# Input projection of a hybrid encoder block: bank split, lasting value tiles, unit order and weight timing changed

## The chip, the cores and the metric

The kernel runs on 1 core of one Trainium2 chip. The metric is the device time of one execution in microseconds (us), and the time of a kernel is the median of several runs. Five engines work beside each other, each with its own queue that it follows strictly in order: PE (TensorE) multiplies matrices into PSUM banks, DVE (VectorE) and ACT (ScalarE) read PSUM and SBUF, POOL (GpSimd) works on SBUF, and SP (SyncE) mostly issues DMA transfers. POOL issues some DMAs too. A semaphore holds an instruction back until what it needs is there, and whatever stands behind it on its engine is held back with it.

## The reference, cut to what matters

```python
def reference(x, mem, positions, norm_mix_g, w_in, ...):           # x: 2048 x 1024
    xn = rmsnorm(h, norm_mix_g[l])
    proj = xn @ w_in[l]                                            # 1024 -> 2560
    q, k, v, u, y = jnp.split(proj, [512, 1024, 1536, 2048], axis=-1)
    q = rope(q.reshape(B, S, 8, 64), positions)
    k = rope(k.reshape(B, S, 8, 64), positions)
    attn = dilated_mixture_attention(q, k, v)                      # three windows and dilations
    uc = centred_depthwise_conv(u, conv_w[l], conv_b[l])           # width 4
    rec = bidirectional_rglru(uc, rg_a_w[l], ...) * jax.nn.gelu(y) # forward and backward scans
    h = h + jnp.concatenate([attn, rec], axis=-1) @ w_out[l]
    h = h + memory_cross_attention(rmsnorm(h, ...), rmsnorm(memf, ...), wq, wk, wv, wo)
    hid = jnp.square(jax.nn.relu(rmsnorm(h, ...) @ w_mlp_in[l]))
    h = h + hid @ w_mlp_out[l]
    return rmsnorm(h, norm_final_g)
```

The change touches the first part: the projection to q, k, v, u and y, the rotary step, and the convolution and recurrence that run beside it.

## The kernel before, in words

Matrices are multiplied in three passes. Each f32 operand is split into a rounded high part (written by ACT, such as `wh`, `xh`) and the remainder (`wl`, `xl`: operand minus high part), and a product is high x high, high x remainder and remainder x high (`mm3`, lines 119 to 121 by the profile). A helper keeps no result that is remainder x remainder.

The sequence is worked in two blocks of 1024 positions, each in two halves of 512 (`th`). The 2560 output columns are cut into ten units of 256 columns: two of u, two of y, and v, k and q with two each (`n2` 0 and 1, that is heads 0 to 3 and 4 to 7). Block 0 makes u and y first. Then block 1 is loaded, keys and values of the memory are made (`memory_kv`), and block 1 makes u, y and its six units of v, k and q. Then x of block 0 is loaded again (`x_block` through the three `wraw` buffers, 16 pieces) and block 0 makes its six units of v, k and q. After that attention begins, head by head, with loads of q, k and v from DRAM (`load_head`; POOL issues those of q and k).

- A u, y, k or q unit is four groups of 24 matmuls of 512 columns (`out_unit`), each into one PSUM bank. A v unit (`v_unit`) also fills four banks, with 48 matmuls of 256 columns each. Banks `m0`, `m1` and `b` hold two each and are taken in turn, six in all; the recurrence's gates use the two banks of `a`.
- DVE evacuates. k and q go through `rope` (lines 376 to 386: four products that read the banks, then two sums, then remainders `rl`, with ACT's `rh` between), and `rh` and `rl` are stored to DRAM from two buffers each. v is scaled by the row norms (line 451) and put as f16 high part (ACT, line 456) and remainder (DVE, line 457) into the tile `vb`, one buffer, whose two columns of ones POOL writes each time (line 454), and stored.
- Weights come by DMA in four pieces of a unit, ACT makes `wh` (line 225), and POOL and DVE make `wl` (line 226) for every other piece. Of `wh` and `wl` there are buffers for two units. The v units of block 1 also sum the squares of their weights' columns over the same pieces (`vss`, `vsq`), which they need before their first bank can be evacuated.
- The recurrence (`lru`) is a generator of 64 pieces: convolution of a chunk (`conv`: POOL takes the first tap at line 489, DVE three more at line 491), the gates of a direction (`gates`: six matmuls into two banks of `a`, then tanh, tanh, exp, tanh and square on ACT, two steps on DVE), `forward` (square root on ACT, products and a scan on DVE, line 531) and `backward` (scan at line 536, sum of the directions by POOL at line 539, product with gelu(y) by DVE at line 544). From block 1's y units on, each step of a unit (four a unit) draws pieces: `due` grows by 1.3 a step, and one piece is drawn for each whole.

A scheduler puts each engine's instructions in order from the written order, priorities and buffers; the queues follow that order. At the change from projection to attention the eight banks are given out again (`psum_phase`): the first attention scores use banks `a`, of which one was a projection bank `m1` before.

Of the kernel before, what the change touches and what calls it, by code (L numbers as in the profile page):

```python
# [24 lines left out]
VW = 130  # L25
# [14 lines left out]
def hybrid_block(ctx: ExitStack, tc: tile.TileContext, prm, x, xT, mem, memT, pos, masks, w_in, gate_w,  # L40
# [35 lines left out]
    turn = {"mm": 0, "mmb": 0}  # L76
# [25 lines left out]
    nhalf = small("nhalf", [P, 4])  # L102
    pool.memset(nhalf, -0.5)
    ones = small("ones", [P, 1])
    pool.memset(ones, 1.0)
    all1 = small("all1", [P, P])
    pool.memset(all1, 1.0)
    dsc = small("dsc", [P, 4])
    hpi = small("hpi", [P, 1])
# [94 lines left out]
    psum_phase("psum1", m0=2, m1=2, a=2, b=2)  # L204
    sh = ExitStack()
    with ExitStack() as s12:
# [10 lines left out]
        def unit_steps(src, r, sums=None):  # L217
            for kk in range(2):
# [3 lines left out]
                for k in range(0, 4, 2):  # L222
# [3 lines left out]
                    (dve if k else pool).tensor_tensor(l[:, k:k + 2, :], t, f32(h[:, k:k + 2, :]), op=ALU.subtract)  # L226
# [36 lines left out]
        def memory_kv(p1):  # L263
# [12 lines left out]
            for c in range(8):  # L276
                if c % 2 == 0 and c > 0:
                    W = unit_w((w_ck if c < 4 else w_cv)[(c % 4) // 2])
                o = ps("mm")
# [15 lines left out]
                else:  # L295
                    t = ps("b")
# [93 lines left out]
        def out_unit(W, X, c, th):  # L390
            o = ps("mmb")
# [40 lines left out]
        def v_unit(W, X, B, n2, step, sums):  # L432

            for th in range(2):
                for m2 in range(2):
                    o = ps("mmb")
# [16 lines left out]
                    vb = p2.tile([P, 8, VW], F16, tag="vb", name="vb", bufs=1)  # L453
                    pool.memset(vb[:, :, 64:66], 1.0)
# [8 lines left out]
        def lru(lr):  # L463
# [12 lines left out]
            def conv(ct, zc):  # L476
# [12 lines left out]
                pool.tensor_scalar(uc, u[:, 0:512], cw[:, ct, 0:1], cb[:, ct:ct + 1], op0=ALU.mult, op1=ALU.add)  # L489
# [44 lines left out]
            def backward(ct, c):  # L534
# [4 lines left out]
                pool.tensor_tensor(hf, hf, ti, op=ALU.add)  # L539
# [1026 lines left out]
```

## Time and profile before

| what | value |
|---|---|
| time, median of 3 runs | 2870.84 us (2866.83 to 2875.58) |
| time of the profiled execution | 2870.64 us |
| its span, first to last instruction | 2868.9 us |
| granted TensorE clock, mean | 0.952 |
| PE busy in the span | 2585.6 us (90%) |
| DVE busy | 2027.9 us (71%) |
| ACT busy | 1285.1 us (45%) |
| POOL busy | 1256.8 us (44%) |

The projection fills the first 704 us of the span. In what follows this part is cut into stretches at places that the trace shows: 0 to 189 us (block 0's u and y, the memory, block 1's u), 189 to 245.5 us (block 1's y), 245.5 to 615 us (block 1's v, k, q, the reload of x, and block 0's v, k, q and second v), 615 to 704 us (block 0's second k and q until attention runs). A row of a timeline gives the start, the duration, the engine, line and operation, the tiles as out<-in, and in square brackets the idle time of that engine before it and what ended it. A row of groups gives the count, the busy time and the mean in ns, then the idle time ahead of the group. Buffer numbers are left out of names.

### The profile page before, as it was taken

To read this page: it belongs to the slowest core of one execution; us is meant where nothing else is said; L and a number is where in the kernel's file an instruction comes from. 1 tells how busy PE (TensorE), PEld (TensorE's weight loads), DVE (VectorE), ACT (ScalarE), POOL (GpSimd) and SP (SyncE) were. 2 spreads that over 40 slices of the span, in tenths; PEclk is the share of its full clock that TensorE was granted. 3 is DMA by queue.
4 is the path that set the end of the run, shared out by engine and by line. 5 is a ranking of instruction groups with operands and counts; after the bars stand their busy time and mean duration, and the time that the engine had idled before them with its cause. 6 is when DMAs were issued, how large, how long until landed. Compare 5 with 4: busy or idle time off the path is not lost. (4 is left out here: it accounts for less than half of the span.)

```text
span 2868.9 us, 40008 instructions
## 1 busy us (share of the span) xinstructions
PE 2585.6 (90%) x14104; PEld 2186.2 (76%) x14104; DVE 2027.9 (71%) x3376; ACT 1285.1 (45%) x2366; POOL 1256.8 (44%) x884
## 2 busy tenths in 40 slices
PE   8899785884889998999997999899998999999997
PEld 6778675774889998787875788778886777777876
DVE  7547676764778878546578544665548999999997
ACT  6438545452556666335433333433333333333342
POOL 2222121211544442451145555646656766666662
PEclk9999897987889999899998999999999999999999
DMA  6433344336677784653243333343335222212213
GB/s 214 144 125 98 116 113 141 101 106 186 180 184 210 201 206 124 202 170 102 97 159 121 108 113 107 113 144 109 109 114 205 71 84 81 81 67 89 77 49 118
DMA packets 258045, 368.43 MB, mean 128 GB/s; under 512 B 85683, under 2 KB 132019, under 8 KB 254773
## 3 DMA queue, kind: packets, MB, share of 16 engines
q1 hardware_dynamic: 253556, 338.62, 37.4%
q0 software_dynamic: 4288, 27.27, 3.8%
q8 instruction: 111, 1.82, 0.3%
q14 instruction: 90, 0.73, 0.1%
HBM read 251.19 MB, written 114.63 MB: 128 GB/s over the span
## 5 line engine op out<-in xcount | busy, mean ns | idle before, releaser
L1299 ACT ACTIVATE c<-raw 128x512 fp32r<-128x512 f32 x162 | 101.8, 632 | 274.0 <-PE m L120 137.4
L1149 ACT ACTIVATE wh<-wr 128x512 fp32r<-128x512 f32 x128 | 80.9, 632 | 288.9 <-PE m L120 145.9
L1150 POOL TENSOR_TENSOR wl<-wr,wh 128x512 fp32r<-128x512 f32 x96 | 144.7, 1508 | 146.3 <-ACT wh L1149 146.3
L757 ACT ACTIVATE sm<-sm,obp 128x256 f32<-128x256 f32 (+1 forms) x384 | 161.4, 467 | 46.2 <-DVE obp L754 40.0
L1150 DVE TENSOR_TENSOR wl<-ws,wh 128x512 fp32r<-128x512 f32 x96 | 82.2, 856 | 126.5 <-ACT wh L1149 117.6
L754 DVE CUSTOM_DVE_ANT_0 sm<-a,msk 128x256 f32<-128x256 f32 (+1 forms) x384 | 131.0, 371 | 31.3 <-PE a L751 27.5
L226 POOL TENSOR_TENSOR wl<-wraw,wh 128x512 fp32r<-128x512 f32 x48 | 70.3, 1467 | 166.5 <-ACT wh L225 157.6
L1171 DVE TENSOR_TENSOR c<-m,c 128x512 f32<-128x512 f32 x64 | 44.2, 690 | 139.9 <-PE m L121 137.9
L769 ACT ACTIVATE ph<-b 128x512 f16<-128x512 f32 (+1 forms) x192 | 100.4, 523 | 95.2 <-PE b L766 90.3
L119 PE MATMUL m<-xh,wh 128*128 128x512 f32 x328 | 131.3, 400 | 7.4 <-ACT xh L320 7.4
L770 DVE SCALAR_TENSOR_TENSOR pl<-b,ph 128x512 f16<-128x512 f32 (+1 forms) x192 | 114.6, 598 | 28.4 <-ACT ph L769 24.5
L120 PE MATMUL m<-xl,wh 128*128 128x512 f32 x328 | 130.1, 397 | 0.7 <-DVE xl L321 0.7
L121 PE MATMUL m<-xh,wl 128*128 128x512 f32 x328 | 130.5, 398 | 0.0
L1300 POOL TENSOR_TENSOR wh<-raw,c 128x512 fp32r<-128x512 f32 x58 | 94.7, 1648 | 76.6 <-ACT c L1299 71.6
L696 POOL TENSOR_SCALAR kc<-kh 128x1024 fp32r<-128x1024 f32 x32 | 68.5, 2141 | 127.7 <-PE a L750 115.6
L766 PE MATMUL b<-prt,sm 128*128 128x128 f32 x640 | 107.8, 283 | 17.3 <-DVE pl L770 9.3
L750 PE MATMUL a<-kc,qb 128*128 128x256 f32 x256 | 108.5, 425 | 5.9 <-DVE obp L754 5.9
L1172 DVE SCALAR_TENSOR_TENSOR c<-c 128x512 f32<-128x512 f32 x96 | 112.4, 1171 | 1.0
L1149 ACT ACTIVATE wh<-ws 128x512 fp32r<-128x512 f32 x96 | 60.3, 628 | 109.0 <-PE m L120 108.0
L121 PE MATMUL m<-t3h,wl 128*128 128x512 f32 x276 | 107.7, 390 | 1.1 <-POOL wl L1150 1.1
L1300 POOL TENSOR_TENSOR wl<-raw,c 128x512 fp32r<-128x512 f32 x58 | 93.3, 1625 | 19.8 <-ACT c L1299 19.8
L751 PE MATMUL a<-kc,qb 128*128 128x256 f32 x256 | 101.6, 397 | 0.0
(571 smaller groups left out, 9731.0 us busy)
## 6 DMA issues: line engine op xcount, KB each, us to landing
wr<-in_w_m SPq DMA_DIRECT2D x64, 512.0 KB
hid_d<-c SPq DMA_DIRECT2D x128, 256.0 KB
wraw<-in_w_in SPq DMA_DIRECT2D x80, 256.0 KB
raw<-in_w_m SPq DMA_DIRECT2D x33, 512.0 KB
rawt<-hid_d SPq DMA_DIRECT2D x26, 512.0 KB
t0h<-hid_d SPq DMA_DIRECT2D x26, 512.0 KB
o_d<-obp SPq DMA_DIRECT2D x16, 528.0 KB
obr<-o_d SPq DMA_DIRECT2D x16, 528.0 KB
```

The costliest lines, as they stand in the source:

```text
L119: pe.matmul(o, ah, bh, start=start, stop=False, **kw)
L120: pe.matmul(o, ah, bl, start=False, stop=False, **kw)
L121: pe.matmul(o, al, bh, start=False, stop=stop, **kw)
L750: pe.matmul(so, q0, kh[:, w0:w0 + 256], start=True, stop=False)
L754: dve.tensor_tensor_reduce(out=sm, in0=sps[:, 256 * z + o0:256 * z + o0 + kw], in1=msk[:, m:m + kw], op0=ALU.add, op1=ALU.min, scale=1.0, ...
L757: exps.append(act.activation(sm, sm, AF.Exp, scale=-1.0, bias=self.obp[:, oc, 65:66]))
L766: pe.transpose(pt[:, c0:c0 + 128], self.sm[:, z, 128 * g:128 * g + 128], idt)
L770: dve.scalar_tensor_tensor(self.pl[:, :w], pt[:, :w], 1024.0, self.ph[:, :w], op0=ALU.mult, op1=ALU.subtract)
L1149: act.activation(h, self.a[n], AF.Copy)
L1150: last[n % 2] = (pool if n % 2 else dve).tensor_tensor(l, self.a[n], f32(h), op=ALU.subtract).ins
L1172: dve.scalar_tensor_tensor(z, z if n < 6 else o, 0.0, z, op0=ALU.max, op1=ALU.mult)
L1300: self.eng[n].tensor_tensor(l[-1], tk, f32(h[-1]), op=ALU.subtract)
```

## The change

- The projection has four banks of its own (`mp`), taken in turn, and the gates and small sums four (`a`), in place of six and two. The banks of attention are the same in number, but given out in another order, so that the first scores' banks were gate banks before.
- The value tile is two tiles that last (`vbs`); their ones are written once.
- In each block the second v unit comes last: v0, k0, q0, k1, q1, v1 in place of v0, k0, q0, v1, k1, q1.
- Each unit but the value units of block 1 has its weights made during the unit before it, a piece at each step. Block 0's last unit gets its weights during the one before it as well (`ahead`).
- POOL makes all weight remainders but those of the two value units of block 1. POOL no longer takes the first tap (ACT does) nor the sum of directions (DVE does, in halves).
- A step draws 1.5 recurrence pieces, not 1.3.
- `ones` and a few constants share tiles.

```diff
-            tag = ("m0", "m1", "b")[turn[tag] % (2 if tag == "mm" else 3)]
+            tag = ("m0", "m1")[turn[tag] % 2]
...
-    psum_phase("psum1", m0=2, m1=2, a=2, b=2)
+    psum_phase("psum1", a=4, mp=4)
...
-                    (dve if k else pool).tensor_tensor(l[:, k:k + 2, :], t, f32(h[:, k:k + 2, :]), op=ALU.subtract)
+                    (dve if k and sums else pool).tensor_tensor(l[:, k:k + 2, :], t, f32(h[:, k:k + 2, :]), op=ALU.subtract)
...
         def out_unit(W, X, c, th):
-            o = ps("mmb")
+            o = ps("mp")
...
-                    vb = p2.tile([P, 8, VW], F16, tag="vb", name="vb", bufs=1)
-                    pool.memset(vb[:, :, 64:66], 1.0)
+                    vb = vbs[(2 * th + m2) % len(vbs)]
...
-                pool.tensor_scalar(uc, u[:, 0:512], cw[:, ct, 0:1], cb[:, ct:ct + 1], op0=ALU.mult, op1=ALU.add)
+                act.activation(uc, u[:, 0:512], AF.Identity, scale=cw[:, ct, 0:1], bias=cb[:, ct:ct + 1])
...
-                pool.tensor_tensor(hf, hf, ti, op=ALU.add)
                 for z in range(2):
                     sl = slice(512 * z, 512 * z + 512)
+                    dve.tensor_tensor(hf[:, sl], hf[:, sl], ti[:, sl], op=ALU.add)
...
-        QKV = [(4, "v", 0), (6, "k", 0), (8, "q", 0), (5, "v", 1), (7, "k", 1), (9, "q", 1)]
+        QKV = [(4, "v", 0), (6, "k", 0), (8, "q", 0), (7, "k", 1), (9, "q", 1), (5, "v", 1)]
...
             def pace():
-                due[0] += 1.3
+                next(nxt[0], None)
+                due[0] += 1.5
...
-                W = first if n == 0 and first else unit_w(w_in[wi], sums=vs)
+                if W is None:
+                    vs = norms(kind)
+                    W = unit_w(w_in[wi], sums=vs)
+                nW = nvs = None
+                if n + 1 < len(units) and units[n + 1][1] != "v":
+                    nW, nxt[0] = unit_w(w_in[units[n + 1][0]], True)
+                elif n + 1 < len(units) and B == 0:
+                    nW, nxt[0] = unit_w(w_in[units[n + 1][0]], True)
...
-            block(0, X, tabs, QKV[:-1], side)
+            W = block(0, X, tabs, QKV[:-1], side, ahead=QKV[-1])
...
-        block(0, X, tabs, QKV[-1:], none)
+        block(0, X, tabs, QKV[-1:], none, W)
...
-        psum_phase("psum2", m0=2, r=1, a=3, b=2)
+        psum_phase("psum2", a=3, b=2, m0=2, r=1)
```

The change moves instructions in every queue. Three places matter below. The rows are engine queues in program order; the line numbers of the changed kernel are a few lower or higher than those of the profile.

ACT, the first y unit of block 1, before: `e` is gelu of y, `tr`, `ti`, `av`, `q` belong to the gates, and ACT_TABLE_LOAD changes the function table.

```order
L411 ACT_TABLE_LOAD
L411 ACTIVATE e<-e 128x512 x2
L513 ACTIVATE tr<-a,gbh 128x512
L411 ACTIVATE e<-e 128x512
L516 ACTIVATE ti<-a,gbh 128x512
L517 ACT_TABLE_LOAD
L517 ACTIVATE av<-tr,nsp_154 128x512
L513 ACTIVATE tr<-a,gbh 128x512
L518 ACTIVATE tr<-tr,sp_153 128x512
L519 ACTIVATE q<-av 128x512
L516 ACTIVATE ti<-a,gbh 128x512
```

The same place of the changed kernel:

```order
L410 ACT_TABLE_LOAD
L410 ACTIVATE e<-e 128x512
L511 ACTIVATE tr<-a,gbh 128x512
L410 ACTIVATE e<-e 128x512
L514 ACTIVATE ti<-a,gbh 128x512
L515 ACT_TABLE_LOAD
L515 ACTIVATE av<-tr,nsp_151 128x512
L516 ACTIVATE tr<-tr,sp_150 128x512
L517 ACTIVATE q<-av 128x512
L511 ACTIVATE tr<-a,gbh 128x512
L410 ACT_TABLE_LOAD
L410 ACTIVATE e<-e 128x512
```

Gelu and gates now alternate one by one: in block 1's y units there are 15 table loads where there were 10.

DVE, block 0, behind the first v unit, before: the tables of cosine and sine (`cosT`, `sinT`) for the rotary step are made, and the first pair of k is read, with recurrence steps (L544, L521, L520) and remainders (`wl`) between; the rows are the end of the second table.

```order
L226 TENSOR_TENSOR wl<-wraw,wh 128x512
L364 TENSOR_SCALAR an<-an 128x512
L521 SCALAR_TENSOR_TENSOR ti<-ti,uc 128x512
L366 SCALAR_TENSOR_TENSOR an<-an 128x512
L368 TENSOR_TENSOR sinT<-n,rbn 128x512
L520 SCALAR_TENSOR_TENSOR q<-q,tr 128x512
L369 TENSOR_TENSOR cosT<-an,rbn 128x512
```

The same place of the changed kernel:

```order
L363 TENSOR_SCALAR an<-an 128x512
L365 SCALAR_TENSOR_TENSOR an<-an 128x512
L367 TENSOR_TENSOR sinT<-n,rbn 128x512
L519 SCALAR_TENSOR_TENSOR ti<-ti,uc 128x512
L368 TENSOR_TENSOR cosT<-an,rbn 128x512
```

One recurrence step and no remainder stand between the parts of the two tables now.

POOL, the end of block 0's units, before: the last remainders and sums of directions, then the loads of head 0 (`qb`, `kh`, `kl`), a regrouping of its keys (`kc`), and the loads of head 1.

```order
L454 MEMSET vb 128x8x2 x2
L226 TENSOR_TENSOR wl<-wraw,wh 128x512 x2
L539 TENSOR_TENSOR ti<-ti 128x1024 x2
L175 DMA qb<-q_d_64 128x2048
L178 DMA kh<-k_d_66 64x2048 x2
L178 DMA kl<-k_d_66 64x2048 x2
L696 TENSOR_SCALAR kc<-kh 128x1024
```

The same place of the changed kernel:

```order
L225 TENSOR_TENSOR wl<-wraw,wh 128x512 x20
L174 DMA qb<-q_d_64 128x2048
L225 TENSOR_TENSOR wl<-wraw,wh 128x512 x3
L177 DMA kh<-k_d_66 64x2048 x2
L177 DMA kl<-k_d_66 64x2048
L225 TENSOR_TENSOR wl<-wraw,wh 128x512
L177 DMA kl<-k_d_66 64x2048
L716 TENSOR_SCALAR kc<-kh 128x1024
```

Three remainders of the last v unit stand between the loads of head 0's queries and keys, and one before its last key load; the regrouping and the loads of head 1 follow behind.

More of the change, by code (lines that the diff above doesn't have):

```diff
@@ L74, in hybrid_block @@
     vm_d = dt_("vm_d", [2, P, 2, 512])
-    turn = {"mm": 0, "mmb": 0}
+    turn = {"mm": 0}
     banks = {}
@@ L101, in hybrid_block @@
     cb, gb, lm, ifq = (col(n) for n in ("conv_b", "gate_b", "lam", "invf"))
-    nhalf = small("nhalf", [P, 4])
+    misc = small("misc", [P, 8])
+    nhalf, hpi = misc[:, 0:4], misc[:, 4:5]
     pool.memset(nhalf, -0.5)
-    ones = small("ones", [P, 1])
-    pool.memset(ones, 1.0)
     all1 = small("all1", [P, P])
     pool.memset(all1, 1.0)
+    ones = all1[:, 0:1]
     dsc = small("dsc", [P, 4])
-    hpi = small("hpi", [P, 1])
     pool.memset(hpi, TWO_PI / 4)
@@ L572, in hybrid_block, with block @@
         U, Y = [(0, "u", 0), (1, "u", 1)], [(2, "y", 0), (3, "y", 1)]
-        QKV = [(4, "v", 0), (6, "k", 0), (8, "q", 0), (5, "v", 1), (7, "k", 1), (9, "q", 1)]
-        def block(B, X, tabs, units, side, first=None, sums=None):
+        QKV = [(4, "v", 0), (6, "k", 0), (8, "q", 0), (7, "k", 1), (9, "q", 1), (5, "v", 1)]
+        def block(B, X, tabs, units, side, first=None, sums=None, ahead=None):
             rbn, cosT, sinT = tabs
+            units = list(units) + ([ahead] if ahead else [])
+            nxt = [iter(())]
             def pace():
-                due[0] += 1.3
+                next(nxt[0], None)
+                due[0] += 1.5
                 while due[0] >= 1:
@@ L582, in pace, with norms @@
                     next(side, None)
+            def norms(kind):
+                if kind != "v" or B == 0:
+                    return None
+                return RowSum(p2, 1, 256, rings={
+                    "ss": lambda: p2.tile([P, 512], F32, tag="rl", name="vss", bufs=2),
+                    "dg": lambda: p2.tile([P, 512], F32, tag="rl", name="vdg", bufs=2),
+                    "sq": lambda: p2.tile([P, 512], F32, tag="rh", name="vsq", bufs=2)})
+            W, vs = first, None
             for n, (wi, kind, n2) in enumerate(units):
+                if n == len(units) - 1 and ahead:
+                    break
@@ L593, in block @@
-                step = pace
+                if W is None:
[6 more added lines that the diff above has]
+                    nW, nxt[0] = unit_w(w_in[units[n + 1][0]], True)
                 if kind in "uy":
-                    uy_unit(W, X, B, n2, kind, rbn, step, sums if n == 0 else None)
+                    uy_unit(W, X, B, n2, kind, rbn, pace, sums if n == 0 else None)
@@ L596, in block @@
                 elif kind == "v":
-                    v_unit(W, X, B, n2, step, vs)
+                    v_unit(W, X, B, n2, pace, vs)
                 else:
-                    qk_unit(W, X, B, n2, kind, cosT, sinT, step)
+                    qk_unit(W, X, B, n2, kind, cosT, sinT, pace)
+                for _ in nxt[0]:
+                    pass
+                W, vs = nW, nvs
                 if kind == ("y" if B else "v") and n2 == 0:
                     fill_tables(B, rbn, cosT, sinT)
+            return W
@@ L603, in hybrid_block @@
+        vbs = [p2.tile([P, 8, VW], F16, name=f"vb{i}") for i in range(2)]
+        for vb in vbs:
+            pool.memset(vb[:, :, 64:66], 1.0)
         none = iter(())
```

12 lines of the change are left out of this document (3 added, 9 removed).

## The prediction

> **What bounds the kernel now.** The clock over windows comes first. The projection takes 704 of 2869 us, and the change touches nothing behind it but the numbering of banks. Columns: stretch, length, busy time of PE, PE's weight load, DVE, ACT, POOL, granted clock, DMA share, GB/s.
>
> ```profile
> core 0: us, PE busy (x) PEld busy (x) DVE busy (x) ACT busy (x) POOL busy (x), PEclk, DMA share, GB/s
> 0.00:189.00 189.00, 166.14 (x797) 137.27 (x798) 118.37 (x193) 89.49 (x157) 46.64 (x54) 0.96 0.52 167
> 189.00:245.50 56.50, 56.50 (x250) 46.41 (x249) 27.27 (x35) 40.24 (x57) 12.35 (x14) 1.00 0.32 106
> 245.50:615.00 369.50, 285.77 (x1493) 244.12 (x1492) 256.50 (x343) 208.67 (x304) 64.50 (x67) 0.88 0.38 113
> 615.00:704.00 89.00, 50.44 (x233) 41.62 (x231) 45.32 (x56) 15.96 (x23) 22.95 (x20) 0.81 0.61 160
> 704.00:2869.00 2165.00, 2026.79 (x11338) 1716.77 (x11338) 1580.40 (x2752) 930.75 (x1829) 1110.34 (x730) 0.97 0.41 127
> ```
>
> I call the first four stretches A, B, C and D. B (block 1's y) is PE alone: 56.5 of 56.5 us. In C no engine is full: PE 285.8, DVE 256.5, ACT 208.7 of 369.5 us. In D PE has 50 of 89. So C and D are bound by waits, and the second view says whose. Waits of PE in C, then of PE in D, then the DVE waits in C that matter, longest first (total, times, longest):
>
> ```profile
> PE a L119 <- ACT tr L513: 36.8, 4, 11.8
> ...
> PE a L119 <- ACT ti L516: 11.4, 6, 5.0
> ...
> PE a L750 <- DVE t L378: 28.4, 1, 28.4
> PE a L750 <- DVE obp L754: 9.7, 1, 9.7
> ...
> DVE rl L386 <- DMA k_d<-rl: 25.1, 9, 6.5
> DVE xl L321 <- ACT xh L320: 13.8, 3, 9.5
> DVE q L520 <- ACT q L519: 12.7, 7, 7.3
> DVE wl L226 <- ACT wh L225: 12.7, 4, 10.9
> DVE v L451 <- PE m L121: 6.3, 4, 2.6
> DVE svc L153 <- PE a L149: 4.4, 2, 2.5
> ```
>
> PE waits 48.2 us for a gate bank (36.8 + 11.4), and 28.4 us at the end for a projection bank that attention has been given. But DVE hardly waits for PE: 6.3 us and 4.4 us in these rows. It waits for its own stores, for the reload of x and for ACT. So freeing PE does not by itself speed up DVE, and C must be costed by DVE.
>
> **Stretch C, by DVE.** The rows of groups in C (DVE, then POOL), and of D (DVE):
>
> ```profile
> L226 DVE TENSOR_TENSOR wl<-wraw,wh 128x512 fp32r<-128x512 f32 x19 | 13.9, 732 | 12.7 <-ACT wh L225 12.7
> L381 DVE TENSOR_TENSOR t<-t,t 128x512 f32<-128x512 f32 x12 | 8.2, 681 | 0.0
> L457 DVE TENSOR_TENSOR vb<-v,vb 128x512 f16<-128x512 f32 x14 | 11.7, 835 | 1.8 <-ACT vb L456 1.3
> L451 DVE SCALAR_TENSOR_TENSOR v<-m,rsb,svr 128x256 f32<-128x256 f32 x22 | 10.5, 476 | 8.7 <-PE m L121 6.3 <-ACT svr L164 2.3
> ...
> L226 POOL TENSOR_TENSOR wl<-wraw,wh 128x512 fp32r<-128x512 f32 x20 | 30.8, 1546 | 55.0 <-ACT wh L225 50.6 <-DMA v_d<-vb 4.2
> L539 POOL TENSOR_TENSOR ti<-ti 128x1024 f32<-128x1024 f32 x6 | 15.5, 2577 | 14.0 <-DVE ti L536 14.0
> L489 POOL TENSOR_SCALAR uc<-u,prt 128x512 f32<-128x512 f32 x11 | 9.0, 815 | 114.9 <-DVE ti L521 81.8 <-issue 27.1 <-DMA u<-u_d 5.9
> ...
> L536 DVE TENSOR_TENSOR_SCAN ti<-av,ti 128x1024 f32<-128x1024 f32 x2 | 7.6, 3824 | 0.0
> L544 DVE TENSOR_TENSOR gy<-ti,gy 128x512 f32<-128x512 f32 x4 | 5.7, 1458 | 11.1 <-DMA gy<-gy_d 11.1
> L529 DVE SCALAR_TENSOR_TENSOR ti<-q,ti 128x1024 f32<-128x1024 f32 x2 | 2.4, 1224 | 2.5 <-ACT q L526 2.4
> L531 DVE TENSOR_TENSOR_SCAN ti<-av,ti 128x1024 f32<-128x1024 f32 x1 | 2.3, 2340 | 0.0
> ```
>
> In the changed kernel C ends where block 0's second k begins, but the v unit that ran just ahead of it (570 to 615 us) now comes last. DVE's work to there: 256.5 before; less 15 of 19 remainders that go to POOL, 11.0; less the evacuation of that v that lay in C, some 4.0 (5 x 0.476 + 2 x 0.835); plus 16 half sums in place of POOL's, 11.0 at 0.681 (the row of a sum of that size); plus the end of the recurrence, which ran in D and must now be done before k, 18.0 (7.6 + 5.7 + 2.4 + 2.3); less what B takes at 1.5 instead of 1.3 a step: 8 x 0.2 = 1.6 more of 64 pieces, some 5. That is 266.
>
> Idle time of DVE in C is 113.0. What stays: the store waits (25.1), the x reload (13.8 and the 7.3 behind it), the weights of a v unit of block 1, which are still not made ahead (10.9), and its column sums (4.4): 61.5. The other 51.5 hang on small delays between ACT, DVE and POOL, some of which go: POOL no longer sits in front of the first tap and the sum, and a `vb` in flight no longer stops POOL. Bounds for C are thus 266 + 61.5 = 327.5 and 266 + 113 = 379. I take a little above the middle, 355, since the same 64 pieces now run in 0.87 of the steps (1.3 / 1.5) and the two queues that wait for each other, ACT and DVE, stay in order: **-14** (-42 to +9.5).
>
> Within C the four banks can hurt in one place. Before, PE began the third pair of block 0's first k and q at 531.96, while DVE read the first pair only at 552.07, behind the rotary tables:
>
> ```profile
> 531.96 0.40 PE L119 MATMUL b<-xh,wh 128*128 128x512 f32 x1
> ...
> 552.07 0.68 DVE L378 TENSOR_TENSOR t<-m,sinT 128x512 f32<-128x512 f32 x1
> ```
>
> With four banks the third pair waits for that read: 20.8 us at most (552.75 - 531.96). Behind a projection matmul that waits stand the gates in PE's queue, and ACT and the recurrence wait for those. DVE's queue no longer has the remainders between the tables, and DVE is the bound here, so this delay is PE's slack; I count nothing, and it weighs in the slow rival.
>
> **POOL.** It gains 15 remainders in C (23.2 at 1.546) and loses the sums and taps (15.5 + 9.0). Their neighbour matters:
>
> ```profile
> 521.82 2.84 POOL L539 TENSOR_TENSOR ti<-ti 128x1024 f32<-128x1024 f32 x1
> ...
> 522.33 2.88 DVE L544 TENSOR_TENSOR gy<-ti,gy 128x512 f32<-128x512 f32 x1
> 525.47 0.68 DVE L544 TENSOR_TENSOR gy<-ti,gy 128x512 f32<-128x512 f32 x1
> ```
>
> The same product took 2.88 us beside POOL's sum and 0.68 us without. POOL's two-input work goes from 30.8 + 15.5 = 46.3 to 54.0 us, so some 8 us more of DVE's time can be stretched; it is inside the upper bound. The Trainium skill, GPSIMD Engine Reference, section Specifications, says that GpSimd shares its SBUF interfaces with VectorE and contends with instructions that have two SBUF inputs. By that rule alone moving all remainders to GpSimd buys VectorE little: each 0.73 us freed puts 1.55 us of contention beside it. The two rows above agree with it.
>
> **Stretch D.** The changed D holds k1, q1 and v1. A unit is 96 matmuls (a v unit 192 of half width), 21.7 us at B's 56.5 / 250 = 0.226 each, so PE alone needs 65. What DVE did there before:
>
> ```profile
> 683.95 0.69 DVE L386 SCALAR_TENSOR_TENSOR rl<-t,rh 128x512 fp32r<-128x512 f32 x1 [15.31 <-DMA k_d<-rl]
> 689.08 0.69 DVE L386 SCALAR_TENSOR_TENSOR rl<-t,rh 128x512 fp32r<-128x512 f32 x1 [4.44 <-DMA k_d<-rl]
> ...
> 691.49 0.68 DVE L379 TENSOR_TENSOR t<-b,cosT 128x512 f32<-128x512 f32 x1
> ...
> 699.57 0.69 DVE L386 SCALAR_TENSOR_TENSOR rl<-t,rh 128x512 fp32r<-128x512 f32 x1 [4.45 <-DMA q_d<-rl]
> ...
> 664.45 0.58 POOL L175 DMA_DIRECT2D qb<-q_d  x1
> ```
>
> The remainders wait for stores while the loads of head 1 (from 664.45) share the DMA engines. The last rotary read of a bank ends at 692.2, 77 us into D. If all that stays, the last two v banks fill behind it (half a unit, 10.9): 88. The first v products on DVE then follow the last remainder at 700.3, and eight at 0.476 with four at 0.835 make 7.1 us, so attention runs at 93 at worst (+4). At best D is PE's 65 and 4 for the last evacuation: 69 (-20). I take 81, the middle: the v unit lies beside DVE's waits now, and a remainder stands before head 0's last key load on POOL, so head 1's loads come later, beside v stores that nothing waits for. **-8**.
>
> **Stretches A and B.** In B ACT gets 5 more table loads and some 5 taps (at 0.623, the row of a cast):
>
> ```profile
> L411 ACT ACT_TABLE_LOAD x4 | 5.1, 1283 | 0.1
> L225 ACT ACTIVATE wh<-wraw 128x512 fp32r<-128x512 f32 x8 | 4.8, 623 | 4.2 <-PE m L120 2.4 <-DMA wraw<-in_w_in 1.8
> ...
> L226 POOL TENSOR_TENSOR wl<-wraw,wh 128x512 fp32r<-128x512 f32 x22 | 30.9, 1407 | 103.1 <-ACT wh L225 98.6 <-DVE e L409 4.3
> ```
>
> 5 x 1.283 + 5 x 0.623 = 9.5, so ACT has 49.8 of 56.5 us and PE still covers it: 0 to +6 if gates come late, I take +2. In A the last row (POOL, 0 to 190 us) says 1.41 us a remainder: four of them make 5.6 us, and a memory weight unit is 48 matmuls of 256 columns, 5.4 us on PE. So POOL just becomes the pace of four such units: 0 to +8, I take +1.
>
> **Sum.** +1 +2 -14 -8 = -19, against the profiled execution's own 2870.64 (1.7 around its span), which is 0.2 below the median: **2852 us**. All low ends give 0 + 0 - 42 - 20 = -62 (2809); all high ends 8 + 6 + 9.5 + 4 = +27.5 (2898).
>
> **Rivals.**
>
> - *PE was the bound after all.* If the gate banks free the rest, C loses the v unit (21.7) and the 48.2 us of gate waits, and D goes to 69: -90, and at half of the gate waits -66; the case spans 2780 to 2830. For it: PE's waits are the largest rows. Against: DVE's 266 us and its 61.5 us of lasting waits leave at most 42 in C, unless the stores get quicker too. Chance 0.15.
> - *The wait at the end only moves in front of the last v's banks, and C gives nothing* (D 88, C 369): -1 to +2 with A and B, about 2870. For it: 61.5 us of waits have causes that the change leaves. Chance 0.21.
> - *Slower: the recurrence drawn faster makes DVE the bound of C.* DVE was busy 256.5 of 369.5 = 0.694. If the mutual waits keep that share, 266 takes 383 us (+13.8), four banks hand the delay to PE, and D stays at 88 to 93: with A and B +16 to +21, 2887 to 2892. It decides when C's share stays below 0.72 (266 / 369.5), the point where C gains nothing. For it: in order queues, 20.8 us of bank lag above. Against: without the stalls of the x reload and the v weights, 21.1 and 10.9, the old share is 256.5 / 337.5 = 0.76. Chance 0.22.
>
> **How the numbers follow.** My forecast's own case, 2834 to 2861, has 0.42. A difference under 0.3%, 8.6 us, can't be told from none. Faster is the forecast and the first rival, 0.57; same 0.21; slower 0.22. The range reaches to the fast rival's upper part and the slow one: 2812 to 2889.
>
> **What would show it.** In the changed profile: gate waits of PE (`a` on `tr` and `ti`) well below 48 us; the 28.4 us wait at attention's first score gone, and in its place waits of `mp` on rotary reads of a few us; store waits of `rl` still about 25 us in C; POOL's wait for `v_d<-vb` gone; DVE's share of C about 0.75. The forecast is wrong if PE's waits vanish and DVE's share passes 0.82, or if `mp` waits on DVE sum to over 30 us.

## The result, and the profile after

The changed kernel takes 2914.43 us (median of 4 runs, 2911.38 to 2917.22), the kernel before 2872.20 in the same session: a ratio of 1.0149, 95% interval 1.0128 to 1.0169. It is 42 us slower, where the forecast was 2852, 19 us faster. The profiled execution has a span of 2915.5 us against 2868.9.

These are the windows of the changed kernel, cut at the same places of the work: A ends at 201.2, B at the last gate of y (259.0), C at block 0's k1 (595.7), D where attention really starts (721.3).

```profile
core 0: us, PE busy (x) PEld busy (x) DVE busy (x) ACT busy (x) POOL busy (x), PEclk, DMA share, GB/s
0.00:201.20 201.20, 170.81 (x797) 139.93 (x798) 109.05 (x173) 91.13 (x161) 71.90 (x74) 0.94 0.48 158
201.20:259.00 57.80, 57.80 (x255) 47.51 (x253) 22.37 (x30) 45.56 (x59) 8.84 (x9) 1.00 0.25 82
259.00:595.70 336.70, 262.95 (x1322) 222.82 (x1322) 242.69 (x318) 206.14 (x304) 67.21 (x53) 0.88 0.40 115
595.70:721.30 125.60, 77.45 (x397) 66.46 (x397) 56.69 (x78) 20.83 (x32) 27.38 (x23) 0.82 0.49 143
721.30:2915.00 2193.70, 2054.61 (x11338) 1717.16 (x11338) 1576.34 (x2752) 933.32 (x1829) 1108.07 (x730) 0.97 0.40 126
```

Against before: A +12.2, B +1.3, C -32.8, D +36.6, and behind the projection +29 (2193.7 against 2164.9), though PE runs the same 11338 matmuls there. The forecast had put nothing on that last row.

**Behind the projection.** Both programs run the same 14104 matmuls, so the n-th of one can be set against the n-th of the other; how much later it starts is called the lag. The lag is 18.0 us at matmul 2900 (attention), 29.2 at 6700 (end of attention), 26.1 at 8500, then it grows evenly to 46.8 at 13700. The growth is the MLP, matmul 8900 to 11100 of each, of the kernel before and then of the changed one:

```profile
1629.80:2142.00 512.20, 502.71 (x2202) 413.67 (x2202) 275.30 (x320) 180.12 (x318) 295.39 (x193) 0.99 0.33 115
```

```profile
1657.10:2182.00 524.90, 516.35 (x2202) 414.30 (x2201) 270.95 (x320) 181.69 (x318) 293.27 (x193) 0.99 0.32 113
```

The granted clock is 0.99 in both, the other engines run the same number of instructions, and yet the same 2202 matmuls take 12.7 us more. The timeline of PE shows it in single instructions, first of the kernel before, then of the changed one:

```profile
1700.26 0.39 PE L119 MATMUL a<-t5h,wh 128*128 128x512 f32 x1
1700.48 0.39 PE L120 MATMUL a<-t5l,wh 128*128 128x512 f32 x1
1700.71 0.39 PE L121 MATMUL a<-t5h,wl 128*128 128x512 f32 x1
1700.93 0.39 PE L119 MATMUL a<-t5h,wh 128*128 128x512 f32 x1
```

```profile
1700.00 0.39 PE L118 MATMUL m<-t1h,wh 128*128 128x512 f32 x1
1700.24 0.39 PE L119 MATMUL m<-t1l,wh 128*128 128x512 f32 x1
1700.47 0.39 PE L120 MATMUL m<-t1h,wl 128*128 128x512 f32 x1
1700.70 0.39 PE L118 MATMUL m<-t1h,wh 128*128 128x512 f32 x1
```

Each is shown as 0.39 us long, but in these rows they start 0.223 us apart before and 0.233 after. Over the MLP's matmuls (8520 to 13780, gaps of 205 to 250 ns from start to start) the mean is 227.0 ns before and 232.5 after. In the projection it is almost unchanged (226.7 and 226.0).

**Stretch A.** POOL's queue and one row of DVE, in the changed kernel, where block 1's second row norm is made:

```profile
180.01 0.19 POOL L114 TENSOR_SCALAR rsb<-rsb 128x4 f32<-128x4 f32 x1 [2.62 <-DVE rsb L152]
180.28 1.26 POOL L225 TENSOR_TENSOR wl<-wraw,wh 128x512 fp32r<-128x512 f32 x1
181.51 1.00 POOL L115 TENSOR_TENSOR rsb<-rsb,misc 128x4 f32<-128x4 f32 x1
182.53 1.26 POOL L225 TENSOR_TENSOR wl<-wraw,wh 128x512 fp32r<-128x512 f32 x1
```

```profile
182.55 1.78 DVE L159 TENSOR_TENSOR dg<-prt,rsb 128x512 f32<-128x512 f32 x1 [2.63 <-POOL u L479]
```

The same row of the kernel before:

```profile
171.51 0.69 DVE L160 TENSOR_TENSOR dg<-prt,rsb 128x512 f32<-128x512 f32 x1 [1.17 <-POOL u L481]
```

Two small steps of POOL make the root of a row norm. A remainder of 1.26 us now stands between them, and the next one runs beside DVE's `dg`, which takes 1.78 us where it took 0.69 before. PE waits 4.95 us for this `dg`, 2.92 before. Over all of A its waits for `dg` are 16.7 us against 12.3; and its matmuls are busy for 170.8 us against 166.1, at a granted clock of 0.94 against 0.96.

**The first v unit, behind B.** ACT in the changed kernel, without a gap from 240 to 270 us:

```profile
255.18 1.28 ACT L410 ACT_TABLE_LOAD   x1
256.47 0.63 ACT L410 ACTIVATE e<-e 128x512 f32<-128x512 f32 x1
...
264.72 1.28 ACT L515 ACT_TABLE_LOAD   x1
266.01 0.81 ACT L515 ACTIVATE av<-tr,nsp 128x512 f32<-128x512 f32 x1
...
267.96 0.61 ACT L517 ACTIVATE q<-av 128x512 f32<-128x512 f32 x1
268.48 1.66 ACT L224 ACTIVATE wh<-wraw 128x512 fp32r<-128x512 f32 x3
```

The casts of the unit's weights stand behind the recurrence's pieces. In the kernel before, one of them ran well before y's end:

```profile
224.89 0.62 ACT L225 ACTIVATE wh<-wraw 128x512 fp32r<-128x512 f32 x1
```

PE now ends y at 259.0 and starts the v unit at 269.1.

**C and D: PE's waits** in the changed kernel, 245 to 722 us:

```profile
PE mp L118 <- ACT wh L224: 35.7, 4, 16.5
PE mp L118 <- DVE v L450: 24.0, 7, 12.2
PE mp L118 <- DVE t L377: 20.2, 3, 15.7
PE a L118 <- ACT tr L511: 14.8, 5, 7.2
PE a L118 <- ACT ti L514: 12.2, 4, 5.9
PE a L770 <- DVE obp L774: 4.7, 1, 4.7
```

The gate waits fell from 48.2 to 27.0 us and the 28.4 us at attention's first score are gone. In their place PE waits for late weights (35.7), for values to be evacuated (24.0) and for rotary reads (20.2). In D the queues hold each other up; DVE, ACT and SP there:

```profile
633.80 0.69 DVE L542 TENSOR_TENSOR gy<-ti,gy 128x512 f32<-128x512 f32 x1 [9.93 <-DMA gy<-gy_d]
634.41 0.68 DVE L377 TENSOR_TENSOR t<-mp,sinT 128x512 f32<-128x512 f32 x1
```

```profile
658.29 0.63 ACT L384 ACTIVATE rh<-t 128x512 fp32r<-128x512 f32 x1 [11.28 <-DMA k_d<-rh]
674.55 0.63 ACT L224 ACTIVATE wh<-wraw 128x512 fp32r<-128x512 f32 x1 [15.63 <-DMA wraw<-in_w_in]
```

```profile
647.04 13.44 SPq L386 DMA_DIRECT2D k_d<-rh  x1
...
663.09 2.68 SPq L223 DMA_DIRECT2D wraw<-in_w_in  x1
```

A product of the recurrence's tail waits 9.93 us for its load, and the rotary read behind it holds a projection bank: PE's 15.7. A store that waits for its cast keeps SP at one instruction for 13.4 us, the load of the last v's weights stands behind it, and ACT and PE wait for that load.

### The profile page after: what moved, and what is told of

Same layout as the page of the kernel before. It is cut to its first block, busy times and chain, and to the rows that moved or that the text cites. A ratio compares the mean times of both kernels' runs of the same rounds, so it can differ in the third digit from the quotient of the medians.

```text
span 2915.5 us, 39979 instructions
## 1 busy us (share of the span) xinstructions
PE 2623.6 (90%) x14104; PEld 2193.9 (75%) x14104; DVE 2007.1 (69%) x3348; ACT 1297.0 (44%) x2381; POOL 1283.4 (44%) x889
## 5 line engine op out<-in xcount | busy, mean ns | idle before, releaser
L225 POOL TENSOR_TENSOR wl<-wraw,wh 128x512 fp32r<-128x512 f32 x92 | 135.9, 1492 | 356.9 <-ACT wh L224 330.0
L118 PE MATMUL mp<-xh,wh 128*128 128x512 f32 x512 | 206.7, 404 | 23.7 <-DVE t L377 16.5
L119 PE MATMUL mp<-xl,wh 128*128 128x512 f32 x512 | 203.7, 398 | 1.8 <-DVE xl L320 1.8
L120 PE MATMUL mp<-xh,wl 128*128 128x512 f32 x512 | 204.0, 399 | 0.5 <-POOL wl L225 0.5
L777 ACT ACTIVATE sm<-sm,obp 128x256 f32<-128x256 f32 (+1 forms) x384 | 161.9, 468 | 50.7 <-DVE obp L774 43.7
L1191 DVE TENSOR_TENSOR c<-m,c 128x512 f32<-128x512 f32 x64 | 44.2, 690 | 147.1 <-PE m L120 145.0
L118 PE MATMUL mp<-wh,xh 128*128 128x256 f32 x256 | 80.2, 320 | 64.8 <-ACT wh L224 35.7
L118 PEld LDWEIGHTS mp<-xh,wh 128*128 128x128 f32 x512 | 99.5, 194 | 46.7 <-issue 17.6
L119 PEld LDWEIGHTS mp<-xl,wh 128*128 128x128 f32 x512 | 99.2, 194 | 24.9 <-DVE xl L320 3.3
L120 PEld LDWEIGHTS mp<-xh,wl 128*128 128x128 f32 x512 | 98.6, 193 | 22.3 <-POOL wl L225 0.9
L770 PE MATMUL a<-kc,qb 128*128 128x256 f32 x256 | 108.5, 425 | 5.9 <-DVE obp L774 5.8
## 6 DMA issues: line engine op xcount, KB each, us to landing
wr<-in_w_m SPq DMA_DIRECT2D x64, 512.0 KB
raw<-in_w_m SPq DMA_DIRECT2D x33, 512.0 KB
rawt<-hid_d SPq DMA_DIRECT2D x26, 512.0 KB
t0h<-hid_d SPq DMA_DIRECT2D x26, 512.0 KB
```

The lines of the kernel that those rows point to most:

```text
L118: pe.matmul(o, ah, bh, start=start, stop=False, **kw)
L119: pe.matmul(o, ah, bl, start=False, stop=False, **kw)
L120: pe.matmul(o, al, bh, start=False, stop=stop, **kw)
L225: (dve if k and sums else pool).tensor_tensor(l[:, k:k + 2, :], t, f32(h[:, k:k + 2, :]), op=ALU.subtract)
L770: pe.matmul(so, q0, kh[:, w0:w0 + 256], start=True, stop=False)
L777: exps.append(act.activation(sm, sm, AF.Exp, scale=-1.0, bias=self.obp[:, oc, 65:66]))
```

## The experiments

All lags are against the profile of the kernel before, in us; "attention" is what the lag gains from matmul 2900 to 6700, "MLP" from 8500 to 13700. Lags are those of one profile, ratios come from all runs. In the table "64" is the changed kernel with 64 unused bytes (the first experiment), which mends the MLP; parts of the change are put back in it. "Before" is the kernel before with one part of the change put in.

| kernel | median | ratio to before, 95% | lag at 840 (A) | at 2900 | attention | MLP |
|---|---|---|---|---|---|---|
| changed | 2914.4 | 1.0128 to 1.0169 | 12.2 | 18.0 | 11.2 | 20.7 |
| e1: 64 | 2890.1 | 1.0035 to 1.0075 | 10.7 | 18.9 | 9.2 | -4.3 |
| e2: before, constants joined | 2897.0 | 1.0060 to 1.0114 | -1.5 | 5.0 | 0.2 | 20.9 |
| e3: 128 bytes | 2910.8 | one run | 9.3 | 22.0 | 10.7 | 9.0 |
| e4: 32 bytes | 2913.4 | one run | 11.6 | 18.5 | 3.8 | 22.1 |
| e5: 64, remainders back | 2869.8 | 0.9953 to 0.9995 | -2.0 | -0.9 | 1.9 | -2.2 |
| e13: 64, remainders back in A | 2883.5 | 1.0004 to 1.0039 | 2.3 | 10.6 | 5.2 | -2.6 |
| e6: 64, draw 1.3 | 2871.7 | 0.9953 to 1.0001 | 9.3 | -7.4 | 11.3 | 0.5 |
| e7: 64, no weights ahead | 2891.1 | 1.0022 to 1.0070 | 9.8 | 16.6 | 10.1 | -2.1 |
| e8: 64, banks 6 and 2 | 2906.8 | 1.0062 to 1.0128 | 12.2 | 26.8 | 6.4 | -4.3 |
| e10: 64, old unit order | 2891.4 | 1.0048 to 1.0092 | 9.5 | 19.5 | -2.4 | -5.8 |
| e11: 64, tap and sum on GpSimd | 2878.5 | 0.9997 to 1.0033 | 10.4 | 13.6 | 3.5 | -2.3 |
| e9: 64, remainders and draw back | 2846.4 | 0.9882 to 0.9943 | -1.6 | -18.5 | -0.6 | -4.3 |
| e14: e9, banks 6 and 2 | 2860.4 | 0.9916 to 0.9961 | -2.5 | -19.0 | 13.2 | -2.8 |
| e15: e9, no weights ahead | 2858.4 | 0.9911 to 0.9954 | -1.0 | -20.9 | 10.6 | -2.3 |
| e16: e9, tap and sum on GpSimd | 2865.3 | 0.9950 to 0.9993 | -3.6 | -3.3 | 17.0 | -4.5 |
| e18: e9, draw 1.15 | 2857.6 | 0.9916 to 0.9969 | -3.8 | -12.0 | -1.4 | -1.7 |
| e12: before, banks 4 and 4 | 2881.2 | 1.0001 to 1.0039 | -1.6 | 7.4 | 0.9 | 1.4 |
| e17: before, tap on ACT, sum on DVE | 2864.4 | 0.9956 to 1.0001 | -0.4 | -2.9 | -0.9 | -1.7 |

The changed kernel, e1, e3 and e4 are one and the same program up to the MLP, and so they show how far two profiles can differ without a cause: by 2.9 us at matmul 840 (9.3 to 12.2), by 4.0 at 2900 (18.0 to 22.0), by 7.4 over attention (3.8 to 11.2). The medians come from several sessions, in which the kernel before took 2872 to 2877 us; so a difference of two medians is uncertain by some 5 us, and ratios are the better measure.

### The MLP: where the tiles lie

Joining the constants (`misc`, `ones` as a column of `all1`) saves 64 bytes, and every tile on the left side moves down by them; the MLP's weights, on the right side, stay. Without the saving the second value tile does not fit, by just these 64 bytes a partition.

```diff
     jp = s7.enter_context(sb("jp"))
+    jp.tile([P, 16], F32, name="gap")
```

> The changed kernel with one unused tile of 64 bytes put ahead of the tiles of the MLP, nothing else: their addresses are then those of the kernel before again (t0h0 at 18080, in the changed kernel at 18016). The MLP's matmuls start every 226.8 ns in the kernel before and every 229 to 236 ns in the changed one. Theory 1: the spacing depends on where the moving tile lies against the weights, which stay at the same place (wh0 at 208800 in both): spacing back to 226.8, 20.5 us come back, 2894 us (2890 to 2898). Theory 2: it is the numbering of the PSUM banks or the chip: spacing stays, 2914 us (2910 to 2918).

```diff
-    nhalf = small("nhalf", [P, 4])
+    misc = small("misc", [P, 8])
+    nhalf, hpi = misc[:, 0:4], misc[:, 4:5]
...
-    ones = small("ones", [P, 1])
+    ones = all1[:, 0:1]
```

> The kernel before with only the constants joined as in the change (nhalf and hpi in one tile of 8 columns, ones as a column of all1), which moves every tile on the left side down by 64 bytes. Theory 1 (place of the tiles): the MLP's matmuls start every 229 to 236 ns, +20.5 us against the kernel before, 2892 us (2888 to 2897), all of it behind 1584 us. Theory 2 (banks or chip): no change, 2872 us, spacing 226.8.

The second is the kernel before, with this part alone. The third and fourth are the first with 32 and with 8 columns in place of 16.

> As the first run, but with an unused tile of 128 bytes. Theory 1 with a period of 128 bytes: nothing is mended, spacing 229 to 236 ns as in the changed kernel, 2914 us. If any other place than the changed kernel's will do (a clash of two certain tiles, say): spacing 226.8, 2894 us.

> As the first run, but with an unused tile of 32 bytes: the moving tiles then lie 96 bytes off the weights, counted modulo 128, where it was 0 in the kernel before and 64 in the changed one. Theory 1 asks for equal places: spacing stays above 226.8. If only the half of 128 bytes counts in which a tile begins, the tiles at 64 and the weights at 32 lie in different halves: 229 to 236, 2914 us. If a distance of exactly 64 is the bad one: 226.8, 2894 us.

The same stretch of the MLP in e1 and in e2:

```profile
1654.40:2166.40 512.00, 504.47 (x2196) 414.51 (x2196) 273.25 (x320) 178.81 (x317) 295.96 (x192) 0.99 0.34 115
```

```profile
1637.50:2162.50 525.00, 515.94 (x2199) 413.33 (x2198) 268.14 (x318) 181.03 (x316) 292.26 (x192) 0.99 0.33 112
```

They take 512.0 and 525.0 us: the place of the tiles is the cause, shown from both sides, and neither the banks nor the chip. The mean spacing is 227.0 ns in e1, 232.5 in e2, 229.8 with 128 bytes, 233.2 with 32. By the addresses of the first expectation, and counted modulo 256, the moving tiles begin 0 (before, e1), -64 (changed, e2), +64 (e3) and -32 bytes (e4) from the weights. Of these four only 0 is fast; the third run was to show whether a period of 128 holds, and 229.8 against 232.5 says that it does not quite. Nor is the distance all of it: products whose weights lie on the left side too (`c`), and so moved along, start 228.9 to 230.8 ns apart on average in the changed kernel and 227.0 to 227.1 before. Whether the distance or the place itself counts, and by what rule, stays open.

### Parts put back one at a time

```diff
-                    (dve if k and sums else pool).tensor_tensor(l[:, k:k + 2, :], ...
+                    (dve if k else pool).tensor_tensor(l[:, k:k + 2, :], ...
```

> From here on every kernel is the changed one with the 64 unused bytes (2890.1 us, its attention's matmul 2900 at 736.6 against 717.7 in the kernel before), with one part put back. Here: every second remainder goes to VectorE again. In the changed kernel stretch A ends 12.2 us later than before (matmul 840 at 211.1 against 198.9), in steps of 2 to 5 us at waits for dg and for the first remainders on DVE. Theory 3 (GpSimd's queue now holds 72 us of work in A against 47, and with it the row sums' small steps and DVE's two-input work come later): A gives back 6 to 12 us, 2880 us (2876 to 2886). Rival (the four banks or the scheduling of the weights ahead shift A): under 3 us back in A, 2888 to 2893, or worse where DVE is short in C.

It gave 20.3 us by the medians and 23 by the ratios, more than expected: 12.7 in A, and 19.8 by attention's start. PE's waits for `dg` up to 245 us fall from 16.3 us in e1 to 10.0. The next run puts them back until the recurrence begins, and keeps GpSimd for the rest:

```diff
+                    (dve if k and (sums or not late[0]) else pool).tensor_tensor(l[:, k:k + 2, :], ...
...
             side = lru(lr)
+            late[0] = True
```

> The changed kernel with the 64 unused bytes; every second remainder on VectorE only until the recurrence begins (the first 189 us), all of them on GpSimd from there. Putting all of them back gave 20.3 us and A ended 11 us sooner. If the cost is A's alone and the rest is passed on: 2872 to 2876 us. If half of it is the rest (VectorE's two-input work stretched beside GpSimd in C): 2877 to 2883.

The time is at the edge of the second case. The lag at 2900 fell by 8.3 of the 19.8, so the larger half of the cost lies in the later units.

```diff
-                due[0] += 1.5
+                due[0] += 1.3
```

> The recurrence drawn 1.3 a step again. In the changed kernel ACT is without a gap from 240 to 270 us (table loads of 1.28 us among the pieces) and the first v unit's weight casts come 10.1 us late (PE at 269.1). Theory 4 (the faster draw fills ACT in B): that wait falls under 3 us, but about 9 of 64 pieces are left over for the end, where they stand in front of k1's and q1's products: 2884 us (2878 to 2892). Rival (the recurrence must end somewhere, and PE's idle time only moves): 2888 to 2896.

It gave 18.4 us (22 by the ratios), again more than expected. The wait in front of the first v is gone: the lag at matmul 1200 is 10.2 against 27.8 in e1. The end did not get longer, against the expectation that left-over pieces would stand there; the lag at 2900 fell by 26.3.

> No weights made a unit ahead in block 1 and block 0's last pass: each unit's weights are asked for at its own start, as before. Theory 5 (drawn piece by piece the loads stand in SP's queue among the stores, and the last v's weights come at 675 us, 15.6 us after ACT is free for them): the end gains 9 to 15 us, the middle loses as much where units then begin with a cast: 2885 us (2876 to 2895). Rival (ahead is what saves the middle): waits of mp for wh pass 50 us (35.7 in the changed kernel from 245 to 722 us), 2900 us or more.

`nW` stays None here, so a unit asks for its weights at its own start. The time differs by 1 us from e1's and the projection's end by 2.3, both within the noise. The time lies in theory 5's range, but its mechanism does not show: the end did not gain 9 us. The rival is out: the waits for `wh` are 44.1 us, and the time is below 2900.

```diff
-    psum_phase("psum1", a=4, mp=4)
+    psum_phase("psum1", m0=2, m1=2, a=2, b=2)
```

> Banks of the projection 6 and 2 again (m0, m1, b in turn, two for the gates). Theory 6 (the forecast's): the gate waits come back, 27 to about 60 us of PE's waits for tr and ti, and the 20.2 us for rotary reads go: 2890 us (2880 to 2900). Rival (the four banks hand DVE's delays to PE and are the cause of the slower end): 2870 to 2879.

With m0, m1 and b taken in turn as before it is 16.7 us slower by the medians and 11 by the ratios, whose intervals overlap; in the profile the projection ends 7.9 later. So the rival is out, and the four banks do not make this kernel slower. In the profile the gate waits are 32.7 us against 26.8 in e1, the waits for rotary reads 3.8 against 20.3, and those for values 40.1 against 24.9: the banks decide where PE waits more than how long.

```diff
-        QKV = [(4, "v", 0), (6, "k", 0), (8, "q", 0), (7, "k", 1), (9, "q", 1), (5, "v", 1)]
+        QKV = [(4, "v", 0), (6, "k", 0), (8, "q", 0), (5, "v", 1), (7, "k", 1), (9, "q", 1)]
```

> The changed kernel with the 64 unused bytes and the units in the old order (second v third, k1 and q1 last). Theory 7 (the forecast's: a v unit at the end lies beside VectorE's store waits): the 28.4 us wait for a rotary read comes back at attention's first score, and the end is 10 us slower: 2900 us (2894 to 2906). Rival (the v unit at the end waits for its late weights and for banks behind the remainders, 21 us in the changed kernel): 2878 to 2888.

Neither theory holds: there is no difference beyond the noise (1.3 us in the median, 0.6 at the projection's end), so no worth of the unit order shows.

```diff
-                act.activation(uc, u[:, 0:512], AF.Identity, scale=cw[:, ct, 0:1], bias=cb[:, ct:ct + 1])
+                pool.tensor_scalar(uc, u[:, 0:512], cw[:, ct, 0:1], cb[:, ct:ct + 1], op0=ALU.mult, op1=ALU.add)
...
+                pool.tensor_tensor(hf, hf, ti, op=ALU.add)
...
-                    dve.tensor_tensor(hf[:, sl], hf[:, sl], ti[:, sl], op=ALU.add)
```

> The changed kernel with the 64 unused bytes and the recurrence's two GpSimd steps back on GpSimd (first tap, sum of both directions). Theory 8 (these 24.5 us of GpSimd's work cost VectorE 11 us and ACT 10 us of queue where both are short): 2884 us (2878 to 2889). Rival (GpSimd is now full of remainders, so taps and sums come later there): 2892 to 2900.

As expected it gave 11.6 us, at the first v again (lag at 1200: 15.7 against 27.8 in e1).

### Together

e9 is e1 with the diffs of e5 and e6.

> Both together: the changed kernel with the 64 unused bytes, every second remainder on VectorE and 1.3 a step. The one alone gave 20.3 us (A's 12 us and what follows), the other 18.4 us (the late first v, 17.2 us in matmul 1200's lag, then a shorter end). Theory: they act in different places, so they add up: 2890 - 20 - 18 = 2852 us (2847 to 2858). Rival: both only free VectorE's and ACT's queues in C, and the second gives little more than the first: 2866 to 2872.

The time is 2846.4 us. Together they give 43.7 us, and singly 20.3 and 18.4 (by the ratios 41, and 23 and 22): within the noise they add up. This version is 0.9% faster than the kernel before. Its waits of PE, 245 to 720 us:

```profile
PE mp L118 <- DVE v L450: 41.8, 9, 25.1
PE mp L118 <- ACT wh L224: 30.8, 3, 20.9
PE a L118 <- ACT tr L511: 16.2, 4, 9.3
PE mp L118 <- DVE t L377: 9.0, 1, 9.0
```

e8's and e7's diffs, now on e9:

> The version with remainders and draw put back (2846 us), with the banks 6 and 2 as before. Alone in the kernel before the four gate banks gave nothing (2881 against 2874), in the changed kernel putting 6 and 2 back cost 17 us. If four gate banks are worth something only with the other parts of the change (weights ahead, second v last): 2860 to 2868 us. If the 17 us came from the overfull queues: 2844 to 2852.

> The version with remainders and draw put back (2846 us), without weights made ahead. In the full queues of the changed kernel they made no difference (2891 against 2890). If that was because ACT and GpSimd had no time for them: now they count, 2856 to 2866 us without. If units never waited for anything else than the v units' weights, which are not made ahead: 2842 to 2850.

By their medians both parts seem worth 12 to 14 us; by the ratios it is 6 to 8, and the intervals overlap with e9's. The profiles say otherwise: the projection ends as early as in e9 (lag -19.0 and -20.9 against -18.5), and the loss stands in attention, which these parts do not touch. There DVE waits for the reload of a head's partial results; e15's row, then e9's:

```profile
DVE mn L844 <- DMA obr<-o_d: 21.3, 4, 9.9
```

```profile
DVE mn L844 <- DMA obr<-o_d: 7.5, 3, 4.2
```

In nine of the table's 19 profiles attention loses 6 to 17 us against the kernel before. Over 690 to 1140 us this row has 15.3 to 28.0 us in those nine, and 8.0 to 14.1 in the other ten and the kernel before. So the loss is mostly this wait: in the changed kernel 11.0 us more of it, and 11.2 lost. There one such reload was issued beside a load of keys of POOL, and DVE's step started only at 1007.66:

```profile
994.58 0.37 SPq L830 DMA_DIRECT2D obr<-o_d  x1
```

```profile
994.64 0.59 POOL L177 DMA_DIRECT2D kh<-k_d  x1 [9.67 <-PE a L771]
```

The other profiles bear this out. In 20 cases POOL issued such a load within 0.5 us of a reload, and in 19 of them the reading step of DVE started 12.3 to 16.6 us after the reload's issue (7.6 in one). In the 66 cases where POOL's load came 0.9 us later or more it was 4.2 to 7.9 us. Between 0.5 and 0.9 us both occur. In eight profiles two reloads took over 12 us, and there attention loses 9.2 to 17.0 us; in the eleven others it was one or none, and attention loses -2.4 to 6.4. That is timing alone; no run moved the load. The changed kernel, e1 and e3 have two such reloads each and e4, the same program up to there, has one: chance decides in part. So what the profile says of the projection and what the median says of a part can differ by 10 us and more, and for banks and weights ahead only the first is tied to the part.

e11's diff on e9:

> The version with remainders and draw put back (2846 us), with the recurrence's first tap and sum on GpSimd as well. In the changed kernel that gave 11.6 us, 12 us of them at the late first v (matmul 1200 at 284.8 against 296.8). That wait is gone here already, so if it was ACT's full queue: 2842 to 2850 us. If VectorE's 11 us count in C by themselves: 2832 to 2840.

Both cases miss: it is worse by 19 us in the median, and the intervals do not overlap. In the profile the projection ends 15.2 us later, and attention loses 17.0 by the reloads. So in this kernel tap and sum belong on ACT and DVE where the queues are free; where ACT is overfull (e11) they do not.

```diff
-                due[0] += 1.3
+                due[0] += 1.15
```

> The version with remainders and draw put back, drawn 1.15 a step instead of 1.3. From 1.5 to 1.3 the projection's end came 17.6 us sooner (matmul 2900 at 716.8 and 699.2). If fewer pieces in the early steps go on helping: 2834 to 2842 us. If the pieces left over (a ninth of 64, 7) now stand in front of the last units: 2846 to 2860 us, matmul 2900 at 699 to 712.

The second case holds: the early part gets faster (lag -24.8 at matmul 1920 against -9.1 in e9), and the end gives it back (-12.0 against -18.5 at 2900). Of the three, 1.3 has the lowest median; its interval overlaps with that of 1.15.

### Alone in the kernel before

The bank edit of the change alone, then the recurrence's two steps alone (the reverse of e8's and e11's diffs):

> The kernel before with one part of the change alone: four banks for the projection's products and four for the gates. Putting this part back cost the changed kernel 17 us. Theory: the gates' 48.2 us of waits in C fall to about 15, and since C is held by VectorE and ACT the gain is 10 to 20 us: 2858 us (2850 to 2864). Rival (the forecast's slow case, DVE's rotary delays go through four banks to PE): 2872 to 2885.

The rival's range holds: 2881.2 us. PE's waits there, 245 to 720 us:

```profile
PE a L119 <- ACT tr L513: 24.4, 4, 18.5
PE a L750 <- DVE t L379: 22.1, 1, 22.1
PE mp L119 <- DVE v L451: 20.8, 8, 7.4
PE mp L119 <- ACT wh L225: 20.4, 2, 12.7
PE mp L119 <- DVE t L378: 13.7, 4, 5.3
```

The gate waits fell by 12.4 (24.4 against 36.8, by `tr`), and 13.7 for rotary reads and 7.2 more for values came in their place (20.8 against 10.4 + 3.2).

> The kernel before with one part of the change alone: the recurrence's first tap on ACT and its sum in halves on VectorE. Taking this part out of the version with remainders and draw put back moved attention's matmul 2900 from 699.2 to 714.3. If the part is worth those 15 us by itself: matmul 2900 at about 703 (717.7 in the kernel before), 2859 us (2853 to 2866). If it takes the other parts (two value tiles, second v last) to be worth something: 2868 to 2880 us.

The gain is 8 us in the median and 2.9 at the projection's end, with an interval that touches no change: whether this part gains alone is not settled.

## Why the prediction was wrong, step by step

The forecast's sum was -19, the profile has +46, so 65 us are to be explained: 11 in A, nothing in B, -19 in C, 45 in D and 29 behind the projection. C and D belong together, since C put off work into D; together they miss by 26. The steps that failed are thus D's term, the zero behind the projection, and A's term.

- **Behind the projection, 0: it measured +29.** Of this 20.7 us lie in the MLP, from the 64 bytes, and about 8 in attention and behind it: 11.2 lost there, with 11.0 more of waits for the reloads, of which 3 come back. The prediction named the bank numbers there and passed over the constants, though the diff shows them. An edit was read as no work and so as no time.
- **A, +1 (0 to +8): +12.2.** POOL was costed as the pace of the memory's units alone. The steps of the row norms stand in the same queue, and DVE's `dg` runs beside the remainders at 1.78 us for 0.69. The prediction had a row that shows such a stretching (2.88 us beside 0.68) and used it for C only. That the remainders are the cause is shown by e5 and e13; how the 12.2 us divide among these steps is not.
- **B, +2 (0 to +6): +1.3, and 10.1 behind it.** ACT was worked out at 49.8 of 56.5 us and PE took no harm in B, as it says. It did not ask what stands behind those pieces in ACT's queue: the weight casts of the next unit. This is 17.6 us of the lag at matmul 1200 (e6).
- **C, -14 (-42 to +9.5): -32.8, those 10.1 included.** DVE worked 242.7 us of 336.7, 0.72, where 266 of 355 (0.75) was forecast. Part of this was put off: the last scans and products of the recurrence, counted before k1 at 18.0 us, run in D (up to 637 us). And of the 61.5 us of DVE's waits that were to stay, most went: stores of `rl` took 9.7 us for 25.1, the reload of x 2.3 for 13.8.
- **D, -8 (-20 to +4): +36.6, the largest miss of a term.** The term took 81 us on the ground that the v unit lies beside DVE's waits. It measured 125.6, of which these waits of PE make 45: the banks behind rotary reads (15.7 + 3.6), the last v's weights (8.8), its bank (12.2), the first scores (4.7). The loads of weights were never followed through SP's queue, past the stores, and the recurrence's tail was taken to be over.
- **Four banks, "I count nothing":** as a sum nothing here speaks against it. With six and two banks put back the projection ends 7.9 us later (e8) or 0.5 sooner (e14); with four and four alone in the kernel before it ends 7.4 later (e12). As a mechanism the second rival's thought, that the wait only moves in front of other banks, comes nearest, though its time (about 2870) and its terms for C and D did not come: gate waits went from 48.2 us to 27.0, and waits for rotary reads and values from 13.6 (10.4 + 3.2) to 44.2, without the 28.4 at the end.
- **The slow rival** (2887 to 2892) had the sign and one cause: the faster draw costs, 18.4 us in the time. Its mechanism was another, DVE as the bound of C, and C got shorter; it did not have the remainders (20.3) or the MLP.
- **Right:** the gate waits well below 48, the 28.4 us gone, the wait for `v_d<-vb` mostly gone (17.5 us in C, 92 before). Wrong: waits on rotary reads of a few us (they are 20.2) and store waits of `rl` of about 25 us in C (9.7). One of the forecast's own signs of being wrong came true: `mp` waits on DVE for 45.6 us (24.0 + 20.2 + 1.4 by its other read), over 30.

By parts and medians, then: 24.3 us for the place of the tiles, 20.3 for the remainders, 18.4 for the draw. Without these the kernel runs at 2846, against the 2852 of the forecast. That nearness is luck and does not make the working right. Two of the things on which the forecast's C rested, remainders off DVE and pieces drawn earlier, are two of the three costs; and the unit order, the ground of its D, is worth nothing that shows (e10). What e9 gains over the kernel before stands with tap and sum on ACT and DVE, but not with them alone: without them 3.3 of its 18.5 us at the projection's end are left (e16), and by themselves they give 2.9 (e17). The two value tiles were not tried alone.

## What to carry to other kernels

A part that adds no work can still move addresses: set the same stretch of matmuls before and after side by side, even far behind the edit, and look at their spacing before looking for a wait. Costing an engine as busy or idle in a stretch is not enough where queues are in order; for each piece added, name what stands behind it in that queue, weight casts and small norm steps above all. Parts of one change must be put back singly and looked at in a profile, since a step of 10 us elsewhere can pass for the worth of a part; and profiles of one and the same program show how large a step has to be before it is read.

## What was not expected of the hardware

- Matmuls of 512 columns, fed without a wait at a granted clock of 0.99, start 227.0 ns apart on average or 232.5, by 64 bytes in the place of their moving tiles: 20.7 us over the MLP. The Trainium skill, SBUF — State Buffer, section SBUF: two separate sides, says that within the engine side only the port pair of VectorE and GpSimd causes contention and that PE never waits on anyone. That sentence names no dependence on where an operand lies; these runs show that PE's pace has one. Whether PE then waits on another engine or only between its own reads no run here tells.
- A DVE product of two SBUF tiles takes 1.78 us where GpSimd makes remainders beside it and 0.69 where it does not.
- The reload of a head's partial results reached its reader 12.3 to 16.6 us after its issue in 19 of 20 cases where GpSimd issued a load of keys within 0.5 us of it, and 4.2 to 7.9 us where that load came 0.9 us later or more. No run moved the loads.
